# A batched 64x64 matmul: the block diagonal's layout, the order of the casts, and the PSUM banks of the last tile

## The chip, the core and the metric

The kernel runs on one core of a Trainium2 chip. The metric is the device time of one execution in microseconds (us), lower is better. The core has TensorE (PE) for matmuls, with its weight loads shown apart (PEld), VectorE (DVE), ScalarE (ACT) and GpSimd (POOL) for elementwise work and for issuing transfers, and SyncE (SP), which here only issues transfers. [...]

## The reference

1024 independent products of 64x64 matrices, in float32:

```python
def setup_inputs():
    return {
        "a": np.random.randn(1024, 64, 64).astype(np.float32),
        "b": np.random.randn(1024, 64, 64).astype(np.float32),
    }

def reference(a, b):
    return np.matmul(a, b).astype(np.float32)
```

Each input has 16.78 MB, and so has the output.

## The kernel before

The 1024 matrices are cut into 16 tiles of 64 (`n_t`), and for a into 8 pairs of tiles (`n_s`). Within a tile the matrices form 16 groups `g` of four (`h`). One matmul handles a group: its stationary operand (the weights) is a 128x128 block diagonal that holds pieces of four matrices of a, its moving operand is 128x64 from b, in bfloat16.

One pair of tiles of a goes through these steps. `load_a` (L63) brings it in by four transfers on POOL's queue, which convert to bfloat16 on the way. `regroup` (L77) orders it on VectorE. `transpose` (L84) transposes on TensorE pieces that hold two bfloat16 values in each float32 word, four into one PSUM bank `at_ps`, and ScalarE copies them to `at_sb` (L92). `spread` (L97) copies a tile's part, four times 32 partitions x 1024 words, into one of two block-diagonal tiles `at_bd` (L102), whose other places were set to zero once.

A tile of b is loaded by `load_b` (L71), 1 MB, into one of four buffers `b_sb`; tiles 1 and 3 go through ScalarE's queue, the others through SP's. `cast` (L109) converts it to bfloat16 on ScalarE; the last tile's cast is shared between ScalarE and VectorE.

`multiply` (L127) runs a tile in two halves of 8 groups, 32 matmuls each. A half fills `o_ps`, two PSUM banks; there are two such buffers. ScalarE evacuates the first half to `o_sb` in four copies, VectorE the second (L146). For the last tile the unit is a quarter, evacuated by ScalarE and VectorE in turn. Between the two halves stands the call `between()`, which is `advance(t)` (L175): the cast of tile t+1, and the load of tile t+4.

The order within each engine's queue is the order of the program text (`manual_schedule`), and an engine waits at an instruction until its inputs are ready and the buffers it writes are free; later instructions of that engine wait behind it. TensorE, VectorE, ScalarE, POOL and SP run beside each other. In turn t of the main loop (L198) stand: `spread(t + 1)`; on even t a `regroup` and a `load_a`; `multiply(t)` with `advance(t)` inside; one `transpose` of a later pair; and the store of tile t-1 (`store`, `put` at L135, on POOL's queue, HOLD = 2). A block-diagonal tile is free for `spread(t + 1)` when tile t-1's matmuls are done; a `b_sb` buffer is free for tile t+4 when the cast of tile t is done.

In ScalarE's queue the order is so: evacuation of the first half of tile t, cast of tile t+1, two copies out of `at_ps`. In VectorE's: spread of tile t+1, on even t the regroup, evacuation of the second half of tile t.

The layout of a block-diagonal tile is the shape of `at_bd` at L57, `[128, 2, 16, 2, 4, 16]`: j, group g, wl, h, mo. The weights of one matmul are the 128 words (wl, h, mo) of one j and g, of which half u is used: 128 bfloat16 values at a step of 4 bytes.

Of the kernel before, what the change touches and what calls it, by code (L numbers as in the profile page):

```python
# [8 lines left out]
fp32 = mybir.dt.float32  # L9
bf16 = mybir.dt.bfloat16  # L10


@with_exitstack
def kernel(
    ctx: ExitStack,
    tc: tile.TileContext,
    a: bass.AP,
    b: bass.AP,
    out: bass.AP,
):  # L20

    nc = tc.nc
    B, M, K = a.shape  # L30
    _, _, N = b.shape
    assert (M, K, N) == (64, 64, 64) and B % 128 == 0

    n_t, n_s = B // 64, B // 128
    A_AHEAD = 3
    B_AHEAD = 4
    N_BD = 2
    HOLD = 2

    a_v = a.rearrange("(s g h) (mp v) k -> s h g mp (v k)", h=4, g=32, v=16)  # L40
    b_v = b.rearrange("(t g h) (kp u) n -> t (h kp) g (u n)", h=4, g=16, u=2)
    o_v = out.rearrange("(t gh x) (mo w) n -> t (x mo) gh (w n)", gh=8, x=8, w=4)

    consts = ctx.enter_context(tc.tile_pool(name="consts", bufs=1))
    a_pool = ctx.enter_context(tc.tile_pool(name="a_pool", bufs=A_AHEAD))
    b_pool = ctx.enter_context(tc.tile_pool(name="b_pool", bufs=B_AHEAD))
    work = ctx.enter_context(tc.tile_pool(name="work", bufs=2))
    o_pool = ctx.enter_context(tc.tile_pool(name="o_pool", bufs=5))
    t_psum = ctx.enter_context(
        tc.tile_pool(name="t_psum", bufs=4, space=bass.MemoryType.PSUM)  # L50
    )
    o_psum = ctx.enter_context(
        tc.tile_pool(name="o_psum", bufs=2, space=bass.MemoryType.PSUM)
    )

    bd_tiles = [
        consts.tile([128, 2, 16, 2, 4, 16], fp32, name=f"at_bd{i}") for i in range(N_BD)  # L57
    ]
    identity = consts.tile([128, 128], fp32)
    a_tiles, b_tiles, abf_tiles, at_tiles, bbf_tiles = {}, {}, {}, {}, {}  # L60
    held = {}

    def load_a(s):  # L63
        a_sb = a_pool.tile([128, 4, 16, 64], bf16, name="a_sb")
        for h in range(4):
            nc.gpsimd.dma_start(  # L66
                out=a_sb[:, h, :, :].rearrange("p v k -> p (v k)"), in_=a_v[s, h]
            )
        a_tiles[s] = a_sb

    def load_b(t):  # L71
        b_sb = b_pool.tile([128, 16, 128], fp32, name="b_sb")
        queue = nc.scalar if t in (1, 3) else nc.sync
        queue.dma_start(out=b_sb[:], in_=b_v[t])  # L74
        b_tiles[t] = b_sb

    def regroup(s):  # L77
        a_sb = a_tiles.pop(s)
        a_bf = work.tile([128, 16, 4, 64], bf16, name="a_bf")
        nc.vector.tensor_copy(a_bf[:], a_sb[:].rearrange("p h v k -> p v h k"))  # L80
        abf_tiles[s] = a_bf
        at_tiles[s] = work.tile([128, 2, 32, 2, 4, 4], fp32, name="at_sb")

    def transpose(s, j):  # L84
        a_cols = abf_tiles[s][:].rearrange("p v h k -> p v (h k)").bitcast(fp32)
        for wl in range(2):
            at_ps = t_psum.tile([128, 4, 128], fp32, name="at_ps")
            for vo in range(4):
                nc.tensor.transpose(  # L89
                    at_ps[:, vo, :], a_cols[:, 4 * vo + 2 * j + wl, :], identity[:]  # L90
                )
            nc.scalar.copy(  # L92
                at_tiles[s][:, j, :, wl, :, :],
                at_ps[:].rearrange("p vo (g mp) -> p g mp vo", mp=4),
            )

    def spread(t):  # L97
        half = slice(16 * (t % 2), 16 * (t % 2) + 16)
        bd = bd_tiles[t % N_BD]
        for h in range(4):  # L100
            rows = slice(32 * h, 32 * h + 32)
            nc.vector.tensor_copy(  # L102
                bd[rows, :, :, :, h, :].rearrange("p j g wl mo -> p j (g wl) mo"),
                at_tiles[t // 2][rows, :, half, :, :, :].rearrange(
                    "p j g wl mp vo -> p j (g wl) (mp vo)"
                ),
            )

    def cast(t):  # L109
        b_bf = work.tile([128, 16, 128], bf16, name="b_bf")  # L110
        b_sb = b_tiles.pop(t)
        if t < n_t - 1:
            nc.scalar.copy(b_bf[:], b_sb[:])  # L113
        else:
            for gq in range(4):
                rows = slice(4 * gq, 4 * gq + 4)
                if gq % 2:
                    nc.vector.tensor_copy(b_bf[:, rows, :], b_sb[:, rows, :])  # L118
                else:
                    nc.scalar.copy(b_bf[:, rows, :], b_sb[:, rows, :])  # L120
        bbf_tiles[t] = b_bf

    def store(t):
        for piece in held.pop(t):
            piece()

    def multiply(t, between):  # L127
        at_bd = bd_tiles[t % N_BD][:].rearrange("p j g wl h mo -> p j g (wl h mo)")
        at_bd = at_bd.bitcast(bf16).rearrange("p j g (c u) -> p j g c u", u=2)
        b_bf = bbf_tiles.pop(t)  # L130
        last = t == n_t - 1
        o_sb = o_pool.tile([128, 8, 2, 2, 64], fp32, name="o_sb")

        def put(lo, n):
            nc.gpsimd.dma_start(  # L135
                out=o_v[t, :, lo : lo + n, :],
                in_=o_sb[:, lo : lo + n].rearrange("p gh j wl n -> p (gh j wl n)"),
            )

        def evacuate(o_ps, gh, gl, n, copy):  # L140

            for par in range(2):
                for wl in range(2):
                    src = o_ps[64 * wl : 64 * wl + 64, gl : gl + n, par, :, :]
                    dst = o_sb[64 * par : 64 * par + 64, gh : gh + n, :, wl, :]
                    copy(dst, src)  # L146

        for half in range(2):
            o_ps = o_psum.tile([128, 4, 2, 2, 64], fp32, name="o_ps")
            for g8 in range(8):  # L150
                g = 8 * half + g8
                for j in range(2):
                    for u in range(2):
                        nc.tensor.matmul(  # L154
                            o_ps[:, g8 // 2, g8 % 2, j, :],
                            at_bd[:, j, g, :, u],
                            b_bf[:, g, 64 * u : 64 * u + 64],
                            start=(u == 0),
                            stop=(u == 1),
                        )  # L160
                if last and g8 % 4 == 3:
                    gl = g8 // 4 * 2
                    copy = nc.vector.tensor_copy if gl else nc.scalar.copy
                    evacuate(o_ps, 4 * half + gl, gl, 2, copy)
            if not last:
                copy = nc.vector.tensor_copy if half else nc.scalar.copy
                evacuate(o_ps, 4 * half, 0, 4, copy)
            if half == 0:
                between()
        if last:  # L170
            held[t] = [lambda q=q: put(2 * q, 2) for q in range(4)]
        else:
            held[t] = [lambda: put(0, 8)]

    def advance(t):  # L175
        if t + 1 < n_t:
            cast(t + 1)
        if t + B_AHEAD < n_t:
            load_b(t + B_AHEAD)

    with tc.manual_schedule():
        load_a(0)
        for t in range(B_AHEAD):
            load_b(t)
        for bd in bd_tiles:
            nc.vector.memset(bd[:], 0.0)  # L186
        make_identity(nc, identity)
        for s in range(1, A_AHEAD):
            load_a(s)
        regroup(0)  # L190
        transpose(0, 0)
        transpose(0, 1)
        spread(0)
        cast(0)
        regroup(1)
        load_a(A_AHEAD)
        transpose(1, 0)
        for t in range(n_t):  # L198
            s, half = t // 2, t % 2
            if t + 1 < n_t:  # L200
                spread(t + 1)
            if half == 0:
                if s + 2 < n_s:
                    regroup(s + 2)
                if s + 1 + A_AHEAD < n_s:
                    load_a(s + 1 + A_AHEAD)
            multiply(t, lambda: advance(t))
            if half == 0 and s + 1 < n_s:
                transpose(s + 1, 1)
            if half == 1 and s + 2 < n_s:  # L210
                transpose(s + 2, 0)
            if t >= HOLD - 1:
                store(t - HOLD + 1)
        for t in range(n_t - HOLD + 1, n_t):
            store(t)
# [30 lines left out]
```

## Time and profile before

| | |
|---|---|
| median of 4 runs | 139.33 us (139.09 to 139.39) |
| the profiled execution | 139.39 us, of which the span of the profile is 137.4 us |
| mean granted TensorE clock | 0.776 |
| moved | HBM read 33.55 MB, written 16.78 MB |
| busy, share of the span | DVE 80%, ACT 63%, PE 49%, PEld 47%, POOL 32% |

The page cuts the span into 40 slices of 3.4 us; each digit is a busy share in tenths, 9 being 90% or more. In the table of groups a line gives: source line, engine, operation, written and read tiles with their sizes, count; then busy time in us and the mean ns of one; then the engine's idle time just before the group, and what ended most of it. Some further lines that are used below:

```profile
L154 PE MATMUL o_ps<-b_bf,at_bd 128*128 128x64 bf16 x1024 | 47.3, 217 | 39.8 <-ACT b_bf L113 15.1
L92 ACT COPY at_sb<-at_ps 128x512 f32<-128x512 f32 x32 | 17.9, 587 | 20.5 <-PE at_ps L89 20.1
L113 ACT CAST b_bf<-b_sb 128x2048 bf16<-128x2048 f32 x15 | 28.5, 1899 | 1.7 <-DMA b_sb<-in_b_dram 1.4
```

SP's queue issued 14 loads of b, taking 0.7 us each for the early ones and 7.0 to 7.4 us from the one at 63.43 us on. ScalarE's two issues of loads took 0.85 and 4.28 us. The waits of SP's queue for casts add up to 41.0 us in eight, the longest 15.4. In the timeline a line gives start and length in us, engine, source line, operation, count, and in brackets the idle time before it and what ended it.

### The profile page before, as it was taken

The numbers are of one execution on the slowest core, as the hardware profiler recorded it, in microseconds if no ns is written. First come the engines' busy times: TensorE is split into PE (matmuls) and PEld (weight loads), VectorE is DVE, ScalarE is ACT, GpSimd is POOL, SyncE is SP. The second block draws the span as 40 slices with busy tenths as digits, with TensorE's granted clock in tenths as the row PEclk, the third lists the DMA queues.
The fourth block names the chain that finished last, engine by engine and source line by source line (L and its number), as shares of the span: only waits on it lengthen the run. The fifth ranks groups of instructions, "written<-read, shape, count | busy, mean of one in ns | idle before, by whom it ended". The sixth has DMA issues, their size and how long they took to land.

```text
span 137.4 us, 2820 instructions
## 1 busy us (share of the span) xinstructions
PE 68.0 (49%) x1152; PEld 64.3 (47%) x1152; DVE 109.5 (80%) x144; ACT 87.1 (63%) x120; POOL 43.4 (32%) x57
## 2 busy tenths in 40 slices
PE   0000063295957375719572779297129835464510
PEld 0000062294956374619563569296129735453510
DVE  5770034959699999999999999999998999979440
ACT  1030029059899997995899668874986895576400
POOL 6811142733443053505153321123020203030640
PEclk9999999559599959995999555959955995555555
DMA  2999999999999999999999999999999999994593
GB/s 69 299 303 312 303 277 259 210 255 271 234 252 287 391 284 271 343 396 368 274 269 382 396 329 271 292 396 393 400 395 395 394 394 393 383 355 153 163 329 123
DMA packets 17468, 42.12 MB, mean 307 GB/s; under 512 B 1072, under 2 KB 1072, under 8 KB 17456
## 3 DMA queue, kind: packets, MB, share of 16 engines
q0 software_dynamic: 9008, 25.17, 64.6%
q1 hardware_dynamic: 7392, 14.68, 29.9%
q10 hardware_dynamic: 1056, 2.10, 4.2%
q8 instruction: 9, 0.15, 0.4%
q14 instruction: 3, 0.02, 0.0%
HBM read 33.55 MB, written 16.78 MB: 366 GB/s over the span
## 4 chain that ended last, share of the span: by engine, by line
DMA 24%; SPq 22%; DVE 20%; issue 12%; PE 8%; ACT 7%; POOL 3%; POOLq 1%; DVEq 0%
SPq L74 22%; DMA b_sb<-in_b_dram 14%; DVE at_bd L102 10%; DMA a_sb<-in_a_dram 10%; DVE o_sb L146 8%; PE at_ps L89 5%; PE o_ps L154 3%; ACT o_sb L146 3%; ACT b_bf L113 3%; DVE a_bf L80 2%; POOL out_dram L135 2%; ACT at_sb L92 2%; POOL a_sb L66 1%; POOLq L241 1%; DVEq L80 0%
## 5 line engine op out<-in xcount | busy, mean ns | idle before, releaser
L154 PE MATMUL o_ps<-b_bf,at_bd 128*128 128x64 bf16 x1024 | 47.3, 217 | 39.8 <-ACT b_bf L113 15.1
L154 PEld LDWEIGHTS <-at_bd 128*128 128x128 bf16 x1024 | 45.2, 115 | 43.2 <-issue 20.9
L102 DVE COPY at_bd<-at_sb 32x1024 f32<-32x1024 f32 x64 | 47.2, 737 | 7.1 <-ACT at_sb L92 5.1
L146 DVE COPY o_sb<-o_ps 64x512 f32<-64x512 f32 (+1 forms) x68 | 44.7, 657 | 4.0 <-PE o_ps L154 2.1
L146 ACT COPY o_sb<-o_ps 64x512 f32<-64x512 f32 (+1 forms) x68 | 37.7, 554 | 14.4 <-PE o_ps L154 11.1
L135 POOL DMA_DIRECT2D out_dram<-o_sb x19 | 20.9, 1099 | 62.9 <-DVE o_sb L146 26.3
L89 PE MATMUL at_ps<-identity,a_bf 128*128 128x128 f32 x128 | 24.1, 353 | 23.3 <-DVE a_bf L80 23.3
L89 PEld LDWEIGHTS at_ps<-identity,a_bf 128*128 128x128 f32 x128 | 20.1, 187 | 23.5 <-issue 23.5
L92 ACT COPY at_sb<-at_ps 128x512 f32<-128x512 f32 x32 | 17.9, 587 | 20.5 <-PE at_ps L89 20.1
L66 POOL DMA_DIRECT2D a_sb<-in_a_dram x32 | 21.9, 690 | 27.3 <-DMA a_sb<-in_a_dram 24.0
L113 ACT CAST b_bf<-b_sb 128x2048 bf16<-128x2048 f32 x15 | 28.5, 1899 | 1.7 <-DMA b_sb<-in_b_dram 1.4
L80 DVE COPY a_bf<-a_sb 128x4096 bf16<-128x4096 bf16 x8 | 10.1, 1259 | 9.2 <-DMA a_sb<-in_a_dram 9.0
L186 DVE MEMSET at_bd<- 128x4096 f32 x2 | 6.9, 3472 | 2.5 <-PEq L230 1.7
L92 ACT ACT_TABLE_LOAD x1 | 1.3, 1283 | 4.3 <-issue 4.3
L74 ACT MOVE_SHAPE b_sb<-in_b_dram x2 | 0.6, 318 | 1.6 <-issue 0.9
L120 ACT CAST b_bf<-b_sb 128x512 bf16<-128x512 f32 x2 | 1.1, 616 | 0.4 <-DMA b_sb<-in_b_dram 0.4
L118 DVE CAST b_bf<-b_sb 128x512 bf16<-128x512 f32 x2 | 0.8, 424 | 0.7 <-DMA b_sb<-in_b_dram 0.7
masks.py:199 POOL TENSOR_SCALAR_AFFINE_SELECT identity<-identity 128x128 f32<-128x128 f32 x1 | 0.3, 287 | 0.1
masks.py:197 POOL MEMSET identity<- 128x128 f32 x1 | 0.3, 271 | 0.0
L230 POOL MEMSET const-float32-0.0<- 128x1 f32 x1 | 0.1, 93 | 0.3 <-issue 0.3
L230 POOL MEMSET const-bfloat16-1.0<- 128x1 bf16 x1 | 0.1, 95 | 0.0
L230 POOL MEMSET const-uint8-127<- 128x1 uint8 x1 | 0.1, 95 | 0.0
(1 smaller groups left out, 0.1 us busy)
## 6 DMA issues: line engine op xcount, KB each, us to landing
out_dram<-o_sb POOLq DMA_DIRECT2D x15, 1024.0 KB, 17.1
a_sb<-in_a_dram POOLq DMA_DIRECT2D x32, 256.0 KB, 16.1
out_dram<-o_sb POOLq DMA_DIRECT2D x4, 256.0 KB, 4.6
b_sb<-in_b_dram SPq DMA_DIRECT2D x14, 0.5 KB, 19.6
b_sb<-in_b_dram ACTq DMA_DIRECT2D x2, 0.5 KB, 18.3
```

What stands on the lines that cost most here:

```text
L66: nc.gpsimd.dma_start(out=a_sb[:, h, :, :].rearrange("p v k -> p (v k)"), in_=a_v[s, h])
L74: queue.dma_start(out=b_sb[:], in_=b_v[t])
L80: nc.vector.tensor_copy(a_bf[:], a_sb[:].rearrange("p h v k -> p v h k"))
L89: nc.tensor.transpose(at_ps[:, vo, :], a_cols[:, 4 * vo + 2 * j + wl, :], identity[:])
L92: nc.scalar.copy(at_tiles[s][:, j, :, wl, :, :], at_ps[:].rearrange("p vo (g mp) -> p g mp vo", mp=4),)
L102: nc.vector.tensor_copy(bd[rows, :, :, :, h, :].rearrange("p j g wl mo -> p j (g wl) mo"), at_tiles[t // 2][rows, :, half, :, :, :].rearrange(
L113: nc.scalar.copy(b_bf[:], b_sb[:])
L135: nc.gpsimd.dma_start(out=o_v[t, :, lo : lo + n, :], in_=o_sb[:, lo : lo + n].rearrange("p gh j wl n -> p (gh j wl n)"),)
L146: copy(dst, src)
L154: nc.tensor.matmul(o_ps[:, g8 // 2, g8 % 2, j, :], at_bd[:, j, g, :, u], b_bf[:, g, 64 * u : 64 * u + 64], start=(u == 0), stop=(u == 1),)
L186: nc.vector.memset(bd[:], 0.0)
L241: with _tile.TileContext(nc) as tc:
```

## The change

Three things change, and two sizes go with them.

- In the block diagonal the group index `g` moves to the innermost place: `[128, 2, 2, 4, 16, 16]` is j, wl, h, mo, g. `at_sb` follows. A copy of `spread` now has four runs of 256 words (1 KB) on the written side and one run on the read side. The 128 weights of one matmul lie 64 bytes apart. ScalarE's copy out of `at_ps` writes runs of 1 KB and reads words that lie 16 bytes apart, where they lay 512 bytes apart.
- `advance` and `between` go; the cast of tile t+1 and the load of tile t+4 stand right behind `spread(t + 1)`, ahead of `multiply(t)`.
- The last tile's matmuls write into four one-bank buffers of the pool that the transposes use, one for each quarter.
- `load_b` sends tiles 5 and 7 through ScalarE's queue too, and `o_sb` gets a sixth buffer.

```diff
-    o_pool = ctx.enter_context(tc.tile_pool(name="o_pool", bufs=5))
+    o_pool = ctx.enter_context(tc.tile_pool(name="o_pool", bufs=6))
...
-        consts.tile([128, 2, 16, 2, 4, 16], fp32, name=f"at_bd{i}") for i in range(N_BD)
+        consts.tile([128, 2, 2, 4, 16, 16], fp32, name=f"at_bd{i}") for i in range(N_BD)
...
-        queue = nc.scalar if t in (1, 3) else nc.sync
+        queue = nc.scalar if t in (1, 3, 5, 7) else nc.sync
...
-        at_tiles[s] = work.tile([128, 2, 32, 2, 4, 4], fp32, name="at_sb")
+        at_tiles[s] = work.tile([128, 2, 2, 2, 4, 4, 16], fp32, name="at_sb")
...
             nc.scalar.copy(
-                at_tiles[s][:, j, :, wl, :, :],
-                at_ps[:].rearrange("p vo (g mp) -> p g mp vo", mp=4),
+                at_tiles[s][:, :, j, wl, :, :, :],
+                at_ps[:].rearrange("p vo (t g mp) -> p t mp vo g", t=2, mp=4),
             )
...
             nc.vector.tensor_copy(
-                bd[rows, :, :, :, h, :].rearrange("p j g wl mo -> p j (g wl) mo"),
-                at_tiles[t // 2][rows, :, half, :, :, :].rearrange(
-                    "p j g wl mp vo -> p j (g wl) (mp vo)"
+                bd[rows, :, :, h, :, :].rearrange("p j wl mo g -> p (j wl) (mo g)"),
+                at_tiles[t // 2][rows, t % 2, :, :, :, :, :].rearrange(
+                    "p j wl mp vo g -> p (j wl) (mp vo g)"
                 ),
             )
...
         for half in range(2):
-            o_ps = o_psum.tile([128, 4, 2, 2, 64], fp32, name="o_ps")
+            if not last:
+                o_ps = o_psum.tile([128, 4, 2, 2, 64], fp32, name="o_ps")
             for g8 in range(8):
+                if last and g8 % 4 == 0:
+                    o_ps = t_psum.tile([128, 2, 2, 2, 64], fp32, name="at_ps")
...
                         nc.tensor.matmul(
-                            o_ps[:, g8 // 2, g8 % 2, j, :],
-                            at_bd[:, j, g, :, u],
+                            o_ps[:, gl, g % 2, j, :],
+                            at_bd[:, j, :, g, u],
...
-            if half == 0:
-                between()
...
-    def advance(t):
-        if t + 1 < n_t:
-            cast(t + 1)
-        if t + B_AHEAD < n_t:
-            load_b(t + B_AHEAD)
...
             if t + 1 < n_t:
                 spread(t + 1)
+                cast(t + 1)
+            if t + B_AHEAD < n_t:
+                load_b(t + B_AHEAD)
...
-            multiply(t, lambda: advance(t))
+            multiply(t)
```

## The prediction

> **What bounds the kernel now.** I read the page's table of busy slices first, then its costliest groups, the engines' timeline stretch by stretch, and the waits of SP's queue.
>
> ```profile
> DVE  5770034959699999999999999999998999979440
> ...
> DMA  2999999999999999999999999999999999994593
> GB/s 69 299 303 312 303 277 259 210 255 271 234 252 287 391 284 271 343 396 368 274 269 382 396 329 271 292 396 393 400 395 395 394 394 393 383 355 153 163 329 123
> ```
>
> One slice is 3.4 us. Two resources are full at once: the DMA engines from 3 to about 124 us, and VectorE (DVE) from 36 to 120 us. Only the end has room: from 124 us both fall off. The bytes agree: 33.55 MB read and 16.78 MB written at the 395 GB/s of the late slices (no cast there, so bytes moved are bytes of HBM) need 127 us, and the DMA starts at 3; about 132 us with a landing is a floor for this transfer plan, 5 us under the span of 137.4.
>
> ```profile
> L102 DVE COPY at_bd<-at_sb 32x1024 f32<-32x1024 f32 x64 | 47.2, 737 | 7.1 <-ACT at_sb L92 5.1
> L146 DVE COPY o_sb<-o_ps 64x512 f32<-64x512 f32 (+1 forms) x68 | 44.7, 657 | 4.0 <-PE o_ps L154 2.1
> ```
>
> These two groups are VectorE's tile: four copies into the block diagonal (2.75 to 3.0 us), four evacuations (2.75), every second tile a regroup (1.23). In the timeline the second-half evacuations of tiles 1 and 13 end at 41.80 and 119.47: 77.7 us for 12 tiles, **6.47 us a tile**, with gaps of 10 to 30 ns. ScalarE (ACT) needs 5.5 a tile (2.35 evacuation, 1.90 cast, 1.2 copies out of the transposes), TensorE (PE) 3.5 to 5.5. Both have slack there.
>
> The end, from the timeline:
>
> ```profile
> 116.80 1.90 ACT L113 CAST b_bf<-b_sb 128x2048 bf16<-128x2048 f32 x1 [1.41 <-DMA b_sb<-in_b_dram]
> ...
> 120.65 2.35 ACT L146 COPY o_sb<-o_ps 64x512 f32<-64x512 f32 x4 [1.95 <-PE o_ps L154]
> ...
> 123.39 1.14 ACT L120 CAST b_bf<-b_sb 128x512 bf16<-128x512 f32 x2 [0.38 <-DMA b_sb<-in_b_dram]
> ...
> 126.66 1.87 PE L154 MATMUL o_ps<-b_bf,at_bd 128*128 128x64 bf16 x32 [1.59 <-ACT o_sb L146]
> ...
> 130.11 1.01 PE L154 MATMUL o_ps<-b_bf,at_bd 128*128 128x64 bf16 x16 [1.59 <-ACT o_sb L146]
> 131.22 1.73 DVE L146 COPY o_sb<-o_ps 64x256 f32<-64x256 f32 x4 [1.73 <-PE o_ps L154]
> 133.24 0.72 POOL L135 DMA_DIRECT2D out_dram<-o_sb  x1 [2.04 <-DVE o_sb L146]
> ```
>
> The last b lands near 123.3. Then the last tile's matmuls stop three times for a PSUM buffer (1.59 twice in the rows shown), the last evacuation ends at 132.95, its store is issued at 133.24 and the span ends 4.17 later.
>
> **The change, part by part.**
>
> *Layout, the copies.* 64 copies of the same size, now in 1 KB runs. Evacuations of 512 and 256 elements take 688 and 422 ns, so about 156 is fixed. A typical spread copy (median 685) then moves 4 KB in 529 ns, 7.7 B/ns; the regroup (1227, in the timeline) moves 8 KB in 1071, 7.6 B/ns, reading runs of 128 B and writing one of 8 KB. The 64 B runs cost nothing already, so **I take no gain here**. The copies above 685 (up to 992) stand beside POOL's DMA descriptors, which stay. ScalarE's copies from at_ps read PSUM at 512 B steps now and take 587 ns, as the contiguous 580 of L146: so the step of 16 B costs 0. Its 512 elements take 428 ns beside a fixed part (L146's two forms, 580 and 366, give 214 for 256); were each to take twice as long, two copies a tile would add 0.86, inside ScalarE's 1 us of slack.
>
> *Layout, the weights.* This is the price. The 128 columns of a weight load lay 4 B apart and now lie 64 B apart. The rows:
>
> ```profile
> L154 PEld LDWEIGHTS <-at_bd x31: 97/98/99, 111.9 to 112.8; 128*128 128x128 bf16 x31
> ...
> L154 PEld LDWEIGHTS <-at_bd x56: 104/133/133, 124.1 to 130.5; 128*128 128x128 bf16 x56
> ...
> L89 PEld LDWEIGHTS at_ps<-identity,a_bf x8: 140/141/141, 31.6 to 32.4; 128*128 128x128 f32 x8
> ```
>
> The first is at granted clock 1.00, the second at 0.50: 98 = f + c and 133 = f + 2c give c = 35 ns that scale with the clock, 63 that don't. The fp32 loads (141, and 231 at half clock) have c = 90. [...] Pairs of load and matmul start every 29 ns (0.9 us for 31) or 53 ns (half clock), the matmul's pace: the load is hidden. No row shows a 64 B step. [...] VectorE's tile hides PE up to (6.47 - 1.4 for eight transposes, 1.07 to 1.95 by clock) / 64 = **79 ns a pair**. The nearest row is the load's own, 64 of the 64-column matmuls covering it; I take a pair as 30 to 60 ns, that is 0 on the path, and keep both ends: 0, and at 108 ns (64 x 108 + 1.4 - 6.47) x 14 = +26 us.
>
> *Casts and b loads ahead.* On ScalarE the cast of tile t+1 moves in front of the four first-half evacuations of tile t. At the start: copies out of transposes end at 29.18, cast 1 then runs 29.2 to 31.1 while matmuls run anyway (it stood at 32.68), the evacuation 31.1 to 33.45, the next copies end at 34.6 instead of 35.68. VectorE's idle stretch before the spread at 35.71 shrinks by 1.0, and its full stretch keeps that: **-1.0 us**. Later the cast no longer waits for matmuls and evacuation. Cast 7 ran 69.14 to 71.04; with matmuls at 61.1 to 63, transposes to 64.8 and copies to 65.4 it can end at 67.3. SP's wait for casts (41.0 us in eight, of its queue) shrinks, and b loads 6 and 8 to 11 are issued some 3.7 us earlier. From 71 us SP is fed by DMA backpressure alone (7.1 to 7.4 us an issue), so b15 could land near 119.5 instead of 123.3; conserved DMA work would give it back as later stores.
>
> The wait that it adds: behind a cast waiting for b stand the evacuation (whose PSUM buffer the next matmuls need) and two copies. Cast 14 is wanted near 110.3 and b14 lands at 113.0 if 3.7 earlier; evacuation 13 then ends at 117.3 and tile 14's matmuls at 121.1, ahead of VectorE's spread 15 (121.6). If b does not move, cast 14 ends at 118.7 as before.
>
> *b5 and b7 on ScalarE's queue.* Two issues of 0.85 (4.28 with one outstanding) go in front of evacuations 1 and 3; they are issued at about 36.5 and 48.0, 1.9 later than SP did. ScalarE has about 1 us a tile of slack, and tile 4's second half isn't wanted by VectorE until 58.0 while even a 4.28 us stall lets it be ready at 56.9: 0, at most 1 us. The sixth o_sb takes out one wait of 2.4 us on ScalarE, inside its slack: 0.
>
> *Last tile in the four banks of the transposes,* idle by then. The three PSUM stops go. With b15 near 119.5 to 121.5: VectorE spreads until 121.6, casts 0.85, evacuates tile 14 until 125.3, then two quarters of 1.73: 128.8. The store is issued at 129.3 and would end at 133.4; but tile 14 and 15's 2.1 MB, issued from 125.8, need 5.3 us and a landing: about 134. That is -3.4. If b15 still lands at 123.3: casts until 124.5, ScalarE's evacuation of tile 14 until 126.9, VectorE's two quarters after tile 14 until 131.2, store 131.5, end 135.7: -1.7. What is late next is the 2.1 MB of stores. I take a value between: **-2.7**, 134.7 for the span. The profiled execution took 139.39, 0.06 above the median of the four (139.33), so the same sum gives 136.6.
>
> **Rivals.** *B, nothing comes of the order (0.12):* DMA full until 124 speaks for it: what b gains, the stores lose, and the last pieces pile up behind each other. Then only half the smaller tail gain is left, 138.5 to 139.5. Against: the DMA is at 0.29 from 124 to 128, pure waiting.
>
> *C, TensorE becomes the bound (0.28), slower:* the weight loads lose their fast form. [...]
>
> *D, ScalarE's queue stops (0.08), slower:* casts waiting for b in front of evacuations starve VectorE, some 0.4 us in each of tiles 11 to 14, and the issues take their 1 us: 140.5 to 141.5 where the tail gives nothing back. Against: the walk above, where VectorE is never reached.
>
> **Numbers.** The forecast, A, has 0.52: 136.6, its own range 134.5 to 138.8. Low end 133.5 (the floor with the usual 2 us around the span), high end 150 (C without its worst half). About 0.2% is what a measurement tells from none: faster 0.56 (nearly all of A, half of B), same 0.06, slower 0.38 (C, D, some of B).
>
> **What would show it.** L101's mean stays 720 to 740 (a fall to 600 would refute my no gain). The weight load's row: near 98 and 133 is A, a c of 70 or more is C, and then TensorE's slices turn to 9s while VectorE shows gaps. Cast 1 ends near 31, spread 2 starts near 34.7. b15's cast near 120 to 121.5, no PSUM stop in tile 15, last store issued 129 to 131.5. I am wrong above all if the load's cost at 64 B passes its cover.

## The result and the profile after

The changed kernel takes **138.97 us** (median of 43 runs, 138.23 to 139.90) against 139.39 us (64 runs, 138.75 to 139.99) of the kernel before: a ratio of 0.9971, 95% interval 0.9962 to 0.9979, 0.3% faster. The forecast was 136.6, with a range of 134.5 to 138.8. The span of the profiled execution is 137.2 us (137.4 before), its mean granted clock 0.84.

The page's slices of the changed kernel, one digit for 3.4 us:

```profile
DVE  5770033967999999999699999999999999999900
...
DMA  3999999999999999999999999999999999976493
```

VectorE now is full up to the end of its work at 130 us. At the start it has a 7 (31 to 34 us) and then 9s, where it had a 9 and then a 6: its idle microsecond there has only moved. A new 6 stands at 65 to 69 us. The DMA engines still have their gap (the 6 and the 4) before the last stretch. The groups of the same page:

```profile
L157 PEld LDWEIGHTS <-at_bd 128*128 128x128 bf16 x1024 | 66.4, 166 | 19.9 <-DVE o_sb L145 16.3
L157 PE MATMUL o_ps<-b_bf,at_bd 128*128 128x64 bf16 x960 | 64.3, 235 | 15.9 <-DVE o_sb L145 14.4
L101 DVE COPY at_bd<-at_sb 32x1024 f32<-32x1024 f32 x64 | 46.9, 733 | 6.2 <-ACT at_sb L92 4.3
```

The copies into the block diagonal take 733 ns (737 before). The weight load takes 166 ns. It does not follow the clock, as the rows of single stretches show (count, then minimum/median/maximum in ns); the first has clock 1.00, the second 0.50, where before had 98 and 133:

```profile
L157 PEld LDWEIGHTS <-at_bd x32: 145/166/184, 111.3 to 113.3; 128*128 128x128 bf16 x32
...
L157 PEld LDWEIGHTS <-at_bd x54: 139/166/178, 117.9 to 122.0; 128*128 128x128 bf16 x54
```

A pair of load and matmul now takes 64 ns: a half of 32 runs 2.1 us, the 64 pairs of a tile 4.1 to 4.2. What that does to VectorE stands in the timeline, at two places. First the kernel before, VectorE alone:

```profile
31.91 2.79 DVE L146 COPY o_sb<-o_ps 64x512 f32<-64x512 f32 x4
...
35.71 3.27 DVE L102 COPY at_bd<-at_sb 32x1024 f32<-32x1024 f32 x4 [1.00 <-ACT at_sb L92]
...
65.27 2.79 DVE L146 COPY o_sb<-o_ps 64x512 f32<-64x512 f32 x4
```

Then the changed kernel:

```profile
28.71 4.14 PE L157 MATMUL o_ps<-b_bf,at_bd 128*128 128x64 bf16 x64
...
32.88 2.79 DVE L145 COPY o_sb<-o_ps 64x512 f32<-64x512 f32 x4 [0.94 <-PE o_ps L157]
35.71 1.40 DVE L101 COPY at_bd<-at_sb 32x1024 f32<-32x1024 f32 x2
...
61.89 4.24 PE L157 MATMUL o_ps<-b_bf,at_bd 128*128 128x64 bf16 x64 [1.82 <-DVE o_sb L145]
...
66.17 2.80 DVE L145 COPY o_sb<-o_ps 64x512 f32<-64x512 f32 x4 [1.20 <-PE o_ps L157]
```

In tile 0 VectorE waits 0.94 us for the second half, and spread 2 starts at 35.71, as before (where the microsecond before it was ScalarE's copies). In tile 5 TensorE can't begin until VectorE has evacuated tile 4, then needs 4.2 us, while VectorE has only the 3.1 us of spread 6 to do: it waits 1.20. The first half of tile 5 has to wait for VectorE's evacuation because it got the PSUM buffer that VectorE frees last. The trace does not name the buffers, but the starts show it: in tiles 2, 4 and 5 the first half starts 0.06 us after VectorE's evacuation of the tile before, and in no tile of the kernel before does it wait for that. So with the new order of the program these tiles got the two buffers the other way round; below this is called swapped. By what rule the pool chooses was not tested. The end, first of the kernel before:

```profile
119.50 3.09 DVE L102 COPY at_bd<-at_sb 32x1024 f32<-32x1024 f32 x4
...
127.45 1.58 POOL L135 DMA_DIRECT2D out_dram<-o_sb  x2 [6.07 <-ACT o_sb L146]
```

Then of the changed kernel, same view:

```profile
118.43 1.14 ACT L119 CAST b_bf<-b_sb 128x512 bf16<-128x512 f32 x2 [2.30 <-DMA b_sb<-in_b_dram]
...
120.07 3.10 DVE L101 COPY at_bd<-at_sb 32x1024 f32<-32x1024 f32 x4
...
124.00 2.80 DVE L145 COPY o_sb<-o_ps 64x512 f32<-64x512 f32 x4
126.82 3.49 DVE L145 COPY o_sb<-at_ps 64x256 f32<-64x256 f32 x8
127.34 3.00 POOL L134 DMA_DIRECT2D out_dram<-o_sb  x4 [5.38 <-issue]
130.60 0.72 POOL L134 DMA_DIRECT2D out_dram<-o_sb  x1 [0.27 <-DVE o_sb L145]
```

The last cast stands 5 us earlier (123.39 before), tile 15's PSUM stops are gone, and the last store is issued 2.6 us earlier. But spread 15 ends 0.6 later than before (123.17, 122.59), and the store of tile 14, which needs VectorE's evacuation behind that spread, is issued at 127.34 (127.45 before). One-us windows of the changed kernel say why this store counts (columns: window, its length in us, busy us of PE, PEld, DVE, ACT and POOL with their counts, then the granted clock, the DMA share and GB/s):

```profile
127.00:128.00 1.00, 0.29 (x6) 0.15 (x3) 0.97 (x3) 0.90 (x3) 0.66 (x1) 0.76 0.00 0
128.00:129.00 1.00, 0.00 (x0) 0.00 (x0) 0.95 (x3) 0.00 (x0) 1.00 (x3) 1.00 0.17 66
129.00:130.00 1.00, 0.00 (x0) 0.00 (x0) 0.96 (x3) 0.00 (x0) 1.00 (x2) 1.00 1.02 356
...
134.00:135.00 1.00, 0.00 (x0) 0.00 (x0) 0.00 (x0) 0.00 (x0) 0.00 (x0) 0.50 1.00 344
```

No transfer moves at 127 to 128. The store's first packets come some 1.5 us after its issue (0.17 of the window from 128 on); from 129 the 2.1 MB of tiles 14 and 15 drain at 315 to 356 GB/s without a pause, until 135.2, and the span ends 2.0 later. The quarters of tile 15 are all issued long before the end of this drain.

### The profile page after: what moved, and what is told of

Its sections match the earlier page's. It is cut to its first block, busy times and chain, and to the rows that moved or that the text cites. A ratio compares the mean times of both kernels' runs of the same rounds, so it can differ in the third digit from the quotient of the medians.

```text
span 137.2 us, 2815 instructions
## 1 busy us (share of the span) xinstructions
PE 86.9 (63%) x1152; PEld 83.6 (61%) x1152; DVE 109.3 (80%) x144; ACT 85.0 (62%) x122; POOL 40.7 (30%) x57
## 4 chain that ended last, share of the span: by engine, by line
DVE 47%; PE 22%; issue 13%; DMA 10%; POOL 3%; POOLq 1%; ACT 0%; DVEq 0%
DVE o_sb L145 24%; DVE at_bd L101 20%; PE o_ps L157 15%; DMA a_sb<-in_a_dram 10%; PE at_ps L89 7%; DVE a_bf L80 3%; POOL out_dram L134 2%; POOL a_sb L66 1%; POOLq L238 1%; ACT at_sb L92 0%; DVEq L80 0%; POOLq L134 0%; POOLq L227 0%
## 5 line engine op out<-in xcount | busy, mean ns | idle before, releaser
L157 PEld LDWEIGHTS <-at_bd 128*128 128x128 bf16 x1024 | 66.4, 166 | 19.9 <-DVE o_sb L145 16.3
L157 PE MATMUL o_ps<-b_bf,at_bd 128*128 128x64 bf16 x960 | 64.3, 235 | 15.9 <-DVE o_sb L145 14.4
L145 DVE COPY o_sb<-o_ps 64x512 f32<-64x512 f32 x60 | 41.3, 689 | 3.1 <-PE o_ps L157 2.1
L145 ACT COPY o_sb<-o_ps 64x512 f32<-64x512 f32 x60 | 35.3, 588 | 7.0 <-PE o_ps L157 6.5
L89 PE MATMUL at_ps<-identity,a_bf 128*128 128x128 f32 x128 | 22.1, 332 | 23.5 <-DVE a_bf L80 23.5
L89 PEld LDWEIGHTS at_ps<-identity,a_bf 128*128 128x128 f32 x128 | 18.7, 176 | 23.7 <-issue 23.7
L66 POOL DMA_DIRECT2D a_sb<-in_a_dram x32 | 19.9, 627 | 33.3 <-DMA a_sb<-in_a_dram 23.7
L145 ACT COPY o_sb<-at_ps 64x256 f32<-64x256 f32 x8 | 3.0, 370 | 3.0 <-PE at_ps L157 2.9
L157 PE MATMUL at_ps<-b_bf,at_bd 128*128 128x64 bf16 x64 | 4.1, 247 | 1.0 <-DVE at_bd L101 1.0
L145 DVE COPY o_sb<-at_ps 64x256 f32<-64x256 f32 x8 | 3.4, 422 | 0.1
```

Source lines behind the costliest of these rows:

```text
L66: nc.gpsimd.dma_start(out=a_sb[:, h, :, :].rearrange("p v k -> p (v k)"), in_=a_v[s, h])
L89: nc.tensor.transpose(at_ps[:, vo, :], a_cols[:, 4 * vo + 2 * j + wl, :], identity[:])
L157: nc.tensor.matmul(o_ps[:, gl, g % 2, j, :], at_bd[:, j, :, g, u], b_bf[:, g, 64 * u : 64 * u + 64], start=(u == 0), stop=(u == 1),)
```

## Experiments

Each is told with its edit; the kernel that it starts from is named. Every ratio is against the kernel before, measured beside it.

### Which part of the change does what

The first four separate the parts. Two theories stood: that the weights' step takes back what the order brings, or that the stores' drain at the end swallows it.

**The change without its layout** (`e1_old_layout`, from the changed kernel):

```diff
-        consts.tile([128, 2, 2, 4, 16, 16], fp32, name=f"at_bd{i}") for i in range(N_BD)
+        consts.tile([128, 2, 16, 2, 4, 16], fp32, name=f"at_bd{i}") for i in range(N_BD)
...
-                            at_bd[:, j, :, g, u],
+                            at_bd[:, j, g, :, u],
```

(with `at_sb`, the copies out of `at_ps` and `spread` as before).

> The changed kernel with the block diagonal's layout of before (weights 4 bytes apart again); casts ahead, two more loads on ScalarE's queue, sixth o_sb and own PSUM banks stay. Theory W (the weights' 64 byte step makes a pair of load and matmul last 64 ns instead of 29 or 53, and this delays VectorE by 0.97 us at tile 0 and 1.2 us at tile 5): about 2 us less than the changed kernel's 138.97, so 137.0 us, the spread of tile 15 ending near 121.0 instead of 123.17, pairs back at 29 and 53 ns. Rival T (the end is set by the 2.1 MB of stores behind tile 14 and the layout is hidden): 138.9 to 139.1 us.

Measured: 136.78 us (136.59 to 137.21), ratio 0.9826 [0.9803, 0.9849], span 134.7. **The layout costs the changed kernel 2.2 us** (138.97 - 136.78). VectorE's timeline of this kernel at the two places:

```profile
32.15 2.79 DVE L146 COPY o_sb<-o_ps 64x512 f32<-64x512 f32 x4
34.98 1.40 DVE L102 COPY at_bd<-at_sb 32x1024 f32<-32x1024 f32 x2
...
63.93 2.80 DVE L146 COPY o_sb<-o_ps 64x512 f32<-64x512 f32 x4
```

No bracket stands behind either evacuation, so VectorE did not wait, and spread 2 starts 0.73 earlier than before. The two waits of the changed kernel, 0.94 and 1.20, add up to 2.14, close to the 2.2. But not all of the 0.94 is the load's price: tile 0's 64 pairs take 0.69 us longer than here (4.14, 3.45), and in that profile they also began 0.58 later (28.71, 28.13). This start lies between 28.13 and 28.96 in the kept profiles, with no relation to the layout, so 0.94 is the figure of one execution. The buffers of tile 5 are swapped here too (TensorE starts at 60.83, when VectorE is done), but its 64 pairs take 2.69 us, less than the spread.

**The layout alone, from the kernel before** (`e2_layout_only`, the same lines in the other direction):

> The kernel before with the new layout alone. Theory W: weight loads at 165 ns and pairs at 64 ns, TensorE busy some 90 us, but behind VectorE except at the start and in the last tile: 0.5 to 1.5 us slower than before, 139.9 to 140.9 us. Rival T: same as before, 139.4 us. The copies of the spread keep their mean of 730 to 740 ns under both.

Measured: 146.18, ratio 1.0497 [1.0467, 1.0527]. Both theories missed: in the old order the layout costs 7.0 us. The timeline of this kernel:

```profile
78.67 2.20 PE L153 MATMUL o_ps<-b_bf,at_bd 128*128 128x64 bf16 x32 [2.44 <-ACT o_sb L145]
...
80.91 2.79 DVE L145 COPY o_sb<-o_ps 64x512 f32<-64x512 f32 x4 [2.54 <-PE o_ps L153]
```

The second half waits for ScalarE: for the evacuation of the first half, by the 2.44 it takes, so both halves have the same buffer. In the old order the first half itself has waited for the cast just before. The kernel before has the same 2.44 in tiles of this kind, but its halves take 1.1 to 1.9 us instead of 2.1 to 2.2, and VectorE feels almost none of it (0.34 us, in tile 11). Here VectorE stops 2.54, 1.63 and 1.27 us, 5.4 of the 6.3 by which the span is longer.

**The last tile's PSUM banks alone** (`e3_tail_only`, from the kernel before):

```diff
-            o_ps = o_psum.tile([128, 4, 2, 2, 64], fp32, name="o_ps")
+            if not last:
+                o_ps = o_psum.tile([128, 4, 2, 2, 64], fp32, name="o_ps")
...
+                if last and g8 % 4 == 0:
+                    o_ps = t_psum.tile([128, 2, 2, 2, 64], fp32, name="at_ps")
```

> The kernel before with the last tile in its own PSUM banks alone. Theory W with the drain: tile 14's store is still issued at 127.4 because VectorE ends its evacuation at 126.9, and 2.1 MB of stores take 6.3 us from 128.9; only the last pieces' gap goes: 138.9 to 139.3 us. Rival F (the step as the prediction had it, the three stops for a PSUM buffer set the end): 1.7 us less than before, 137.7 us.

Measured: 139.33 against 139.19, ratio 1.0007 [0.9991, 1.0023]: nothing, though its last store is issued at 130.93 instead of 133.24.

**Everything but layout and banks** (`e4_order_only`: casts and loads ahead, b5 and b7 on ScalarE's queue, six `o_sb`; from the kernel before):

> The kernel before with casts and loads of b ahead, tiles 5 and 7 on ScalarE's queue and the sixth o_sb; old layout, last tile in the shared banks. Theory W: VectorE's chain runs 1.0 to 2 us earlier and tile 14's evacuation ends near 124.7; the three stops of the last tile stay, last store issued near 131: 137.3 to 137.8 us. Rival T: no gain, 139.2 to 139.5 us.

Measured: 136.98, ratio 0.9834 [0.9811, 0.9857]. The whole gain is in this part, and the banks add at most 0.2 to it (136.78), within the intervals. Five profiles, put side by side, say what sets the end:

| kernel | tile 14's store issued | last store issued | span | span - first |
|---|---|---|---|---|
| before | 127.45 | 133.24 | 137.4 | 9.9 |
| after | 127.34 | 130.60 | 137.2 | 9.9 |
| banks alone | 127.66 | 130.93 | 137.5 | 9.8 |
| order, old banks | 125.29 | 130.57 | 135.2 | 9.9 |
| without the layout | 124.86 | 128.13 | 134.7 | 9.8 |

In these five the span ends 9.8 to 9.9 us behind the issue of tile 14's store, wherever the last store stands: 1.5 to the first packets, 6.3 of drain, 2.0 to the end of the span. A last store that comes late enough sets the end by itself: in `e2_layout_only` above, and in `e9_casts_only` and two kernels like it below, the span ends 3.9 to 4.0 us behind the last issue, and 11.3 to 13.1 behind that of tile 14's store.

### What the step of the weights costs

With four groups innermost the columns lie 16 bytes apart, with two 8 bytes (`e6_step16`, `e7_step8`, from the changed kernel; `at_sb` and `spread` follow). The edit for 8 bytes follows; for 16 the shape is `[128, 2, 4, 2, 4, 16, 4]`, and `g // 4` and `g % 4` stand for `g // 2` and `g % 2`:

```diff
-        consts.tile([128, 2, 2, 4, 16, 16], fp32, name=f"at_bd{i}") for i in range(N_BD)
+        consts.tile([128, 2, 8, 2, 4, 16, 2], fp32, name=f"at_bd{i}") for i in range(N_BD)
...
-                            at_bd[:, j, :, g, u],
+                            at_bd[:, j, g // 2, :, g % 2, u],
```

> The changed kernel with four groups innermost instead of sixteen: the weights of a matmul lie 16 bytes apart, copies of the spread run 256 bytes. [...]

> [...]

Measured: 138.67 (ratio 0.9954 [0.9939, 0.9970]) for 16 bytes, 136.65 (0.9810 [0.9789, 0.9831]) for 8. The load rows, with 16 bytes at clock 1.00, then with 8 bytes at 1.00 and at 0.50:

```profile
L158 PEld LDWEIGHTS <-at_bd x64: 160/166/167, 28.7 to 32.7; 128*128 128x128 bf16 x64
...
L158 PEld LDWEIGHTS <-at_bd x64: 112/118/134, 92.8 to 96.9; 128*128 128x128 bf16 x64
...
L158 PEld LDWEIGHTS <-at_bd x61: 113/130/133, 117.9 to 122.5; 128*128 128x128 bf16 x61
```

With 16 bytes the load takes 166 ns at full clock, as with 64, and 163 at half clock. With 8 bytes it is 118 and 130, with 4 it was 98 and 133. So at full clock the load is 20 ns longer at 8 bytes than at 4, another 48 at 16, and from 16 to 64 nothing is added; at half clock 8 bytes cost nothing. Why it is so, no run shows. The kernel's time does not feel these 20 ns: it is that of the one at 4 bytes (136.65, 136.78). The copies' mean with 8 bytes is 726 ns, in runs of 128 bytes: no length of run tried makes them faster.

### Where it is paid

If tile 5's wait comes from the swapped PSUM buffers, giving each half its own buffer removes it (`e5_fixed_psum`, from the changed kernel):

```diff
-        tc.tile_pool(name="o_psum", bufs=2, space=bass.MemoryType.PSUM)
+            tc.tile_pool(name=f"o_psum{i}", bufs=1, space=bass.MemoryType.PSUM)
+        for i in range(2)
...
-                o_ps = o_psum.tile([128, 4, 2, 2, 64], fp32, name="o_ps")
+                o_ps = o_psum[half].tile([128, 4, 2, 2, 64], fp32, name="o_ps")
```

> The changed kernel with the two halves of a tile bound to one PSUM buffer each, so that the first half of tiles 2, 4 and 5 no longer gets the buffer that VectorE frees last. Theory W: tile 5's 1.2 us wait of VectorE goes, the wait at tile 0 (0.97 us) stays: 137.6 to 138.0 us. Rival: the long pairs put another wait in its place: 138.8 to 139.1 us.

Measured: 137.61, ratio 0.9890 [0.9869, 0.9911]. Tile 5 in this kernel, TensorE's first half and VectorE's evacuation:

```profile
58.23 2.10 PE L160 MATMUL o_ps<-b_bf,at_bd 128*128 128x64 bf16 x32
...
65.40 2.80 DVE L148 COPY o_sb<-o_ps 64x512 f32<-64x512 f32 x4
```

The first half starts at 58.23 instead of 61.89, and the evacuation has no wait. That returns 1.36 of the 2.2 us. The other 0.83 (137.61 - 136.78) stays; the only wait of VectorE for matmuls that is left is that of tile 0 (1.19 us in this profile, whose matmuls began at 28.91), where no earlier work can cover it.

### Which part of the order does what

**Casts and loads ahead, alone** (`e9_casts_only`, from the kernel before):

```diff
                 spread(t + 1)
+                cast(t + 1)
+            if t + B_AHEAD < n_t:
+                load_b(t + B_AHEAD)
...
-            if half == 0:
-                between()
```

> The kernel before with only the casts and loads of b put ahead of the matmuls: all of tiles 5 and 7 on SP's queue, five o_sb, old layout, shared PSUM banks. Theory: the gain of the order is the cast's place, not the queue or the sixth buffer: 136.8 to 137.4 us, as the fourth experiment's 136.98. Rival: the two loads on ScalarE's queue and the sixth buffer carry half of it: 137.9 to 138.4 us.

Measured: 139.97, ratio 1.0056 [1.0042, 1.0070]: **slower**, which neither theory had. Its timeline:

```profile
113.66 1.90 ACT L113 CAST b_bf<-b_sb 128x2048 bf16<-128x2048 f32 x1 [2.50 <-DMA b_sb<-in_b_dram]
...
121.43 1.14 ACT L120 CAST b_bf<-b_sb 128x512 bf16<-128x512 f32 x2 [3.61 <-DMA b_sb<-in_b_dram]
122.58 2.35 ACT L146 COPY o_sb<-o_ps 64x512 f32<-64x512 f32 x4
...
124.98 1.01 PE L155 MATMUL o_ps<-b_bf,at_bd 128*128 128x64 bf16 x16 [3.78 <-ACT o_sb L146]
```

The cast waits 3.61 us for b, behind it stands the evacuation of tile 14, and behind that, for its PSUM buffer, the last tile's matmuls (3.78). The last store is issued at 134.18, and the span ends 3.9 after it. The early loads alone don't bring b early enough.

**The same with the new layout** (`e10_layout_casts`) asks whether the layout's price depends on the order:

> The same with the new layout. Theory (in the order of before, evacuation, cast and the next first half's matmuls follow one another in a loop of ScalarE and TensorE, 2.36 + 1.90 + 2.2 us with the new layout's pairs, and the cast ahead takes 1.90 out of it): the layout costs about 2 us here instead of 7, 138.7 to 139.4 us. Rival (the long pairs delay VectorE whatever the order; the changed kernel is saved by its other parts): 142 us or more.

Measured: 140.69, ratio 1.0099 [1.0083, 1.0114]. That lies between the two forecasts. The layout adds 0.7 us here, 2.2 in the full change, 7.0 in the old order, with loads of 166 ns on average in each of the last two: one step of the weights, three prices.

**The two sizes, singly.** One theory says that the queue carries the order's gain, its rival that the sixth buffer does. To the casts ahead, b5 and b7 on ScalarE's queue (`e13_casts_queue`) or a sixth `o_sb` (`e14_casts_buffer`); and to the kernel before, the queue alone (`e15_queue_only`):

```diff
-        queue = nc.scalar if t in (1, 3) else nc.sync
+        queue = nc.scalar if t in (1, 3, 5, 7) else nc.sync
```

```diff
-    o_pool = ctx.enter_context(tc.tile_pool(name="o_pool", bufs=5))
+    o_pool = ctx.enter_context(tc.tile_pool(name="o_pool", bufs=6))
```

> The ninth experiment's kernel (casts ahead, all else as before) with the loads of tiles 5 and 7 on ScalarE's queue. Theory Q (two queues give b a larger part of the DMA while both hold loads, so the last b lands some 4 us earlier and no cast waits in front of an evacuation at the end): 136.8 to 137.3 us, last cast near 117 instead of 121.4. Rival O (the sixth o_sb does it): 139.5 to 140.0 us.

> The ninth experiment's kernel with a sixth o_sb and all loads but 1 and 3 on SP's queue. Theory Q: 139.5 to 140.0 us, last cast near 121. Rival O: 136.8 to 137.3 us.

> The kernel before with the loads of tiles 5 and 7 on ScalarE's queue and nothing else. Theory Q with the sum of the tail: b15 lands some 3 us earlier, but VectorE's spread of tile 15 still ends near 122.6, so only 0.7 us go: 138.4 to 138.9 us. Rival (an issue on ScalarE's queue holds up the evacuations behind it): 139.4 us or more.

| casts ahead | queue | sixth `o_sb` | time, us | ratio |
|---|---|---|---|---|
| no | yes | no | 139.46 | 1.0004 [0.9990, 1.0018] |
| yes | no | no | 139.97 | 1.0056 [1.0042, 1.0070] |
| yes | no | yes | 140.25 | 1.0062 [1.0047, 1.0078] |
| yes | yes | no | 139.37 | 1.0001 [0.9986, 1.0015] |
| yes | yes | yes | 136.98 | 0.9834 [0.9811, 0.9857] |

The last row is `e4_order_only`. None of the steps tried alone gains anything, so theory Q and rival O both missed: queue and buffer need each other. (For the queue alone, the rival's 139.4 or more came.) With the queue the casts wait 2.5 us for b instead of 7.3 (3.6 for the last, 3.7 for two before it): SP's loads of b land sooner (median 18.0 us from issue instead of 21.5). But the stores now land later (median 21.2 us instead of 19.1), and with five `o_sb` the evacuations wait for them (7.6 us in two, 3.4 with the casts ahead alone). The timeline of casts and queue:

```profile
98.27 2.35 ACT L146 COPY o_sb<-o_ps 64x512 f32<-64x512 f32 x4 [5.38 <-DMA out_dram<-o_sb]
```

Here ScalarE waits 5.38 us for a store to land. The sixth buffer shortens just this wait (0.89 in the last row) and is worth 2.4 us, but only once the queue has moved the transfers: without the queue it leaves the casts waiting for b (7.6 us in four). The sixth buffer without the casts, and queue and buffer together without them, weren't tried. So it stays open whether the casts ahead are needed for the gain at all.

### The end

If tile 14's store sets the end, cutting it in two lets the first half, which ScalarE has ready early, fill the gap in the DMA's work (`e8_halves`, from the change without its layout):

```diff
-            held[t] = [lambda: put(0, 8)]
+            held[t] = [lambda: put(0, 8)] if t < n_t - 2 else [lambda q=q: put(4 * q, 4) for q in range(2)]
```

> The kernel of the first experiment (old layout, the rest of the change) with tile 14's store cut in two, so that its first half leaves as soon as ScalarE has evacuated it. Theory drain (DMA stands idle for some 3 us ahead of tile 14's store, then needs 6.3 us for 2.1 MB): the 0.5 MB that goes early takes 1.5 us off: 135.1 to 135.5 us. Rival (the last quarter's store is late by itself): 136.6 to 136.9 us.

Measured: **135.05**, ratio 0.9704 [0.9683, 0.9724], 1.7 us less than without the cut. Its windows, columns as above:

```profile
124.00:125.00 1.00, 0.15 (x5) 0.03 (x1) 0.96 (x3) 0.92 (x3) 0.22 (x1) 1.00 1.00 381
125.00:126.00 1.00, 0.00 (x0) 0.00 (x0) 0.97 (x3) 0.00 (x0) 1.00 (x2) 1.00 0.60 225
126.00:127.00 1.00, 0.00 (x0) 0.00 (x0) 0.96 (x3) 0.00 (x0) 0.69 (x2) 1.00 0.95 344
```

Of the gap, one window at 0.60 is left; the first half was issued at 120.34.

To this kernel, one more step each: the last tile's stores on SP's queue, so that they don't stand behind POOL's issues (`e11_halves_sp`, the diff), or a PSUM buffer for each half (`e12_halves_fixed_psum`, the edit told above):

```diff
-            nc.gpsimd.dma_start(
+            (nc.sync if last else nc.gpsimd).dma_start(
```

> The eighth experiment's kernel with the last tile's four stores issued by SP's queue instead of POOL's. Theory (from issue to the first packet POOL's queue takes some 1.5 us, and its issues of 0.7 us each stand one behind the other): the last quarter leaves earlier, 134.4 to 134.9 us against 135.05. Rival (the stores drain at 320 to 350 GB/s whatever the queue): 135.0 to 135.2 us.

> The eighth experiment's kernel with each half of a tile bound to its own PSUM buffer. Theory: with the old layout the pairs are short enough that the odd buffer at tiles 2, 4 and 5 makes VectorE wait for nothing: 134.9 to 135.2 us, no change. Rival: the odd buffer still costs part of the 1.2 us: 134.0 to 134.7 us.

Measured: **134.65**, ratio 0.9672 [0.9659, 0.9686], the fastest version of this study, though its interval just touches that of 135.05; and 134.96, ratio 0.9700 [0.9684, 0.9717], no change: with the old layout the swapped buffer does no harm.

## Why the prediction went wrong

- **The weights: the step that failed.** It read "I take a pair as 30 to 60 ns, that is 0 on the path". The pair takes 64 ns, just outside, and far below the cover of 79: rival C did not come, TensorE is busy 63%. No run shows the 108 ns of the upper end, nor a fast form that the loads could lose; the runs showed a load of 166 ns and the pair of 64. But "0 on the path" does not follow from an average cover, and measured it is 2.2 us. 79 ns was TensorE's share of a mean tile; at tile 0 and tile 5 there is no lead, and the longer pairs are paid there: 1.20 at tile 5 (a buffer for each half brought back 1.36) and some 0.7 of the 0.94 at tile 0. VectorE is full nearly everywhere else and never gives it back. The choice of the nearest row was wrong too: that row has the columns 4 bytes apart (98 ns at full clock), and no row of before had them 16 or more apart, where the runs show 166. Nor is the price a part that scales with the clock: it is 166 ns at both clocks, so neither of the signs named, 98 and 133 or a c of 70, came. Without the layout the kernel takes 136.78, where 136.6 was forecast.
- **The copies** gain nothing, as said: 733 ns, and 726 to 737 at every run length. ScalarE's copies out of `at_ps` take 593 ns (587 before), so their term of 0 held, though the row it was compared with is not contiguous: L146 reads runs of 512 bytes, one out of every 1 KB.
- **The start.** Cast 1 ended at 31.36 (31 forecast) and the copies that spread 2 needs were done at 34.75 (34.6). Without the layout, spread 2 starts at 34.98, 0.73 earlier instead of 1.0; with it, tile 0's wait eats all.
- **b early.** The last cast came at 118.43, earlier than "120 to 121.5". The reason given, SP's waits for casts would shrink, holds only for the casts ahead alone (31.1 us in six, from 41.0 in eight), and that brings the last cast to 121.43. In the full change the waits grew, to 59.0 in eight; it is the second queue that shortens the casts' waits for b (2.5 us instead of 7.3 with the casts ahead alone).
- **The queue and the sixth buffer**, "0, at most 1 us" and "inside its slack: 0", are the second error, though the sum did not show it: together they make the difference between 139.97 and 136.98. The text had the sentence that leads there, that DMA work is conserved and comes back as later stores, but did not carry it to the buffers that later stores hold.
- **Rival B's** range, 138.5 to 139.5, holds the measured 138.97, but that is luck: its reason, that nothing comes of the order, is refuted by 136.98. What it says of b and the stores is what happens with five buffers (139.37).
- **Rival D** had its mechanism right and its place wrong: not 0.4 us in each of tiles 11 to 14, but once, in the last tile (VectorE idle for 3.77 us there in `e9_casts_only`), where it makes the casts ahead alone slower. In the full change the last cast still waits 2.30 us, and VectorE is not reached.
- **The tail**, -1.7 to -3.4, mixed two things. No PSUM stop is left and the last store came at 130.60, in the range named; yet the banks are worth 0. In the kernel before two ends lie together: tile 14's store, 127.45 + 9.8 = 137.25, and the last store, 133.24 + 3.9 = 137.14, with the distances of the other kernels, against a span of 137.4. The banks move only the second. What moves the first is VectorE's evacuation of tile 14, by way of the order. The drain's term was mis-sized: 6.3 us, with 1.5 ahead of it to the first packets, for "5.3 us and a landing". That the kernel without the layout has the span of 134.7 that was forecast is partly luck: its store of tile 14 was issued at 124.86, 0.9 earlier than the 125.8 in the sum.

## What to carry to other kernels

A cost per instruction that an average tile hides is still paid wherever a chain has no lead, so check it at the first tile and at each place where the engine waits for a buffer, not at the mean. Edits that each cost or gain nothing can depend on each other: here a second queue made loads land sooner (median 18.0 us from issue instead of 21.5) and stores later (21.2 instead of 19.1), and was only worth something with a buffer for the stores that then came later. When an end does not move though its last instruction does, look for the issue that keeps a constant distance to the end over several kernels; here that was tile 14's store (9.8 to 9.9 us in five profiles), and cutting it in two brought 1.7 us.

## What the runs showed of the hardware

- A weight load takes 166 ns with its columns 64 bytes apart, at granted clock 1.00 and at 0.50 alike (the changed kernel), and 166 and 163 at 16 bytes (`e6_step16`); at 8 bytes it is 118 and 130 (`e7_step8`), at 4 bytes 98 and 133 (before).
- A pair of load and matmul at 64 bytes takes 64 ns, although the load alone has 166 (the changed kernel): loads overlap each other or the matmuls more than their length shows.
- Stores with nothing beside them, on POOL's queue, drain at 315 to 356 GB/s in the changed kernel, less than the 386 to 407 of its slices from 93 to 120 us, where loads move too.
- From the issue of a store on POOL's queue to its first packets 1.5 us pass on an idle DMA (127.34 to about 128.83 in the changed kernel).
